# Query projection of an eight-head latent attention: rotary columns per head with their swap, or rotary chunks of all heads computed once ahead of the attention

## Chip, cores and metric

One core of one Trainium2 chip runs the whole kernel. The metric is the device time of one execution in microseconds, as the median of several runs.

## What is computed

A decoder block on one sequence of 1024 tokens and 1024 features: two token mixers beside each other (a latent attention with 8 heads and a gated linear attention with 4 heads), merged by sigmoid gates, then a SwiGLU feed-forward of 2816 columns. The change concerns the queries and the rotary key of the latent attention:

```python
q = (rmsnorm(c_q, norm_cq) @ w_uq).reshape(B, S, H, MLA_QK_DIM)      # 384 -> 8 heads x (64 plain + 32 rotary)
q_nope, q_rope = q[..., :64], q[..., 64:]
q_rope = apply_rope(q_rope, cos, sin)      # x1 cos - x2 sin, x2 cos + x1 sin
k_rope = apply_rope(k_rope, cos, sin)      # one rotary key of 32 columns for all heads
k = concat([k_nope, k_rope]); q = concat([q_nope, q_rope]) * 96 ** -0.5
s = causal_mask(q @ k.T); p = softmax(s); o = p @ v
```

## The kernel before, in words

**Products.** All activations are held transposed (features on partitions, tokens along the free axis, in two halves of 512). Every fp32 operand is kept as two fp32r parts, high and low. `split` makes the high part by a cast on ACT and the low part by a subtraction on POOL or DVE, and `mm3` (L134 to L138) makes a product of three matmuls: high x high, high x low, low x high. A matmul here has a moving side of 128x512. The big products (input projection, feed-forward) go through a Strassen-Winograd form in pairs of 128 columns: `weights` loads and splits a weight tile, `p_first` (L204) makes the first product and copies it to SBUF (ACT, L208), and `p_second`, `p_t2`, `p_t3`, `p_t4`, `p_t1`, `p_last` follow; between them plus and minus (DVE, L180 and L181) combine weights and results. A weight tile is split by ACT (L164) and DVE (L165).

**Pools that matter.** Rings of buffers hold these tiles: `st` has 5 buffers (products copied from PSUM and results on their way to DRAM), `wh` and `wl` have 4 each (split weights, and in this part the latents too), `wr` has 4 (raw weights from DRAM), and PSUM has 4 banks for each of two tags in the first part of the program.

**Before the attention.** `latents` (L751) loads the latents from DRAM, squares them (ACT), sums the squares by matmuls against ones (L772), and forms the inverse root on POOL (`rstd_of`, a power, L99). `token_rows` (L777) turns the result into a row that stands on all partitions: DVE makes a diagonal matrix (L782), and a matmul against ones spreads it (L785). The latent of the keys is multiplied by its rows and then split (L795 to L797). The latent of the queries is not multiplied by them: `q_split` (ACT L801, DVE L802) scales it by the gain alone and splits it at once, and the rows enter later, through `tab`.

**Queries.** A head's 96 query columns become 128: 64 plain ones, 32 rotary ones, and the 32 rotary ones again with their halves swapped (`load_uq`, L829, eight small casts and eight subtractions for each pair of heads). `qproj` (L844) makes one head and one half of the tokens by 9 matmuls, multiplies the PSUM bank by `tab` (DVE, L850: rows of the norm on the plain partitions, cosine times norm and signed sine times norm on the rotary ones), casts (ACT, L852) and subtracts (POOL, L853). The key has its rotary part summed and repeated to 64 partitions by `sel` (L870), so that the scores' contraction over 128 partitions adds cosine and sine terms. So the query projection is 8 chunks x 2 halves x 9 = 144 matmuls.

**Attention.** A loop over 32 items (head h, r from 0 to 3), each with 256 queries: `scores` (matmuls into `pss`, a mask matmul L931, a reduce on DVE L933, the exponential on ACT L935) and, one item later, `values` (transposes L950, copies ACT L953 and subtraction DVE L954, matmuls L959, then ACT L967 and DVE L968 into `zraw`, which is stored to `d_oa` at L971 once for each pair of heads). Item r has scores over 256(r+1) keys, so items r = 0 and 1 are small. Projections of later heads and parts of the gated mixer's output (`pj` banks) stand between the items.

**Order of the work.** Each engine runs its instructions in one fixed order. The order is not the written one: a list scheduler of the framework places the instructions of each engine by its own model, and pools of buffers set who must wait for whom. DMAs are issued by SP, in order as well.

Of the kernel before, what the change touches and what calls it, by code (L numbers as in the profile page):

```python
# [10 lines left out]
F32 = mybir.dt.float32  # L11
# [4 lines left out]
ALU = mybir.AluOpType  # L16
# [4 lines left out]
P = 128  # L21
# [27 lines left out]
def block_kernel(ctx, tc, x, positions, ln_mix, w_in, norm_cq, w_uq, norm_ckv, w_ukv, w_oa,  # L49
# [25 lines left out]
    d_oa = dram.tile([512, S], F32, name="d_oa")  # L75

# [451 lines left out]
    rot = rotp.tile([P, S], F32, name="rot", tag="rot", bufs=1)  # L528

    def rotary_table():  # L530
# [6 lines left out]
        nc.gpsimd.memset(frow[:, 1, :].rearrange("p (a r) -> p a r", r=64)[:, :, 32:48], -1.0)  # L537
# [5 lines left out]
        for half in range(2):  # L543
# [12 lines left out]
            nc.scalar.activation(rot[:, hs], ang, AF.Sin, scale=fcol[:, 1:2])  # L556
            nc.scalar.activation(kk, ang, AF.Abs)
            nc.vector.tensor_scalar(kk, kk, -1.0, math.pi / 2, ALU.mult, ALU.add)
            for r in (0, 64):
                nc.scalar.activation(rot[r:r + 32, hs], kk[r:r + 32], AF.Sin)  # L560
# [190 lines left out]
    def latents(row, n, name, each=None):  # L751
# [8 lines left out]
        for half in range(2):  # L760
            sq = None
            for c in range(n):
# [6 lines left out]
                if each:  # L769
                    each(c, half, raw[c][half])  # L770
# [17 lines left out]


    rs_kv, raws = latents(384, 2, "ck")  # L790
    ckh, ckl = ck_t
    for half, ps in enumerate(token_rows(rs_kv)):
        for c in range(2):
            cr = raws[c][half]
            nc.vector.scalar_tensor_tensor(cr, cr, g_ckv[:, c:c + 1], ps, ALU.mult, ALU.mult)  # L795
            nc.scalar.copy(ckh[half][c], cr)
            nc.vector.tensor_tensor(ckl[half][c], cr, ckh[half][c].bitcast(F32), ALU.subtract)  # L797
# [12 lines left out]

# [17 lines left out]

    def load_uq(hp):  # L829
        raw, hi, lo = wtiles(768)  # L830
        nc.sync.dma_start(raw[:, 0:576].rearrange("p (c n) -> p c n", c=3),
                          w_uq[0][:, hp * 192:(hp + 1) * 192].rearrange("(c p) n -> p c n", p=P))
        r4_ = raw[:, 0:576].rearrange("p (c h n) -> p c h n", c=3, h=2)
# [10 lines left out]
    def qproj(h, half, wq, newbank):  # L844
        hs = slice(half * HALF, (half + 1) * HALF)
# [741 lines left out]
```

## Time and profile before

| | |
|---|---|
| runs of the kernel before | 1490.79, 1494.8, 1496.61 us (median 1494.8) |
| the profiled execution | 1490.29 us, of which the span is 1488.6 us |
| PE busy | 1438.9 us (97% of the span) |
| DVE, ACT, POOL busy | 1021.8, 673.5, 491.5 us (69%, 45%, 33%) |
| DMA | 181.51 MB, mean 122 GB/s |
| granted TensorE clock, mean | 0.99 |

The span runs from the first to the last instruction of the profiled execution, and its own time is 1.7 us longer. Busy times are sums over the whole span. Since PE is busy nearly always, the places where it is not, and the number of its matmuls, are what a reader looks at first; a row of the trace then tells for one stretch which wait ended last.

### The profile page before, as it was taken

How to read it: one execution, taken by the hardware profiler on the slowest of the kernel's cores; microseconds unless marked ns; L12 is line 12 of the kernel's file. 1: busy time of each engine (PE TensorE's matmuls, PEld its weight loads, DVE VectorE, ACT ScalarE, POOL GpSimd, SP SyncE). 2: the span in 40 equal slices, each digit the busy share in tenths (PEclk: the TensorE clock that was granted, in tenths of full speed). 3: DMA queues.
4: the chain of work that ended last, by engine and by line, in shares of the span. 5: the costliest groups of instructions: out<-in, count | busy, mean ns of one | idle time of the engine just before them, and what ended most of it. 6: DMA issues, size and time to landing. Idle time of an engine off the chain costs nothing.

```text
span 1488.6 us, 20316 instructions
## 1 busy us (share of the span) xinstructions
PE 1438.9 (97%) x7422; PEld 1209.9 (81%) x7422; DVE 1021.8 (69%) x1453; ACT 673.5 (45%) x1333; POOL 491.5 (33%) x419
## 2 busy tenths in 40 slices
PE   7999999999979999999999899999999999999997
PEld 5899888778858888887899778888888888788886
DVE  4876786979665777574613876666666666886875
ACT  6542364535555776576303632222222223354454
POOL 3312231323122114235713465555555555100000
PEclk9999999999989999999999999999999999999999
DMA  8134324223421014358622223233323234952441
GB/s 237 43 116 128 114 92 147 86 79 109 146 93 59 1 44 143 104 173 282 250 77 86 85 73 105 94 104 107 99 100 106 93 106 148 398 202 94 139 158 57
DMA packets 123158, 181.51 MB, mean 122 GB/s; under 512 B 12898, under 2 KB 76915, under 8 KB 123059
## 3 DMA queue, kind: packets, MB, share of 16 engines
q1 hardware_dynamic: 122482, 178.38, 36.4%
q10 hardware_dynamic: 576, 1.84, 0.3%
q8 instruction: 58, 0.95, 0.3%
q14 instruction: 42, 0.34, 0.1%
HBM read 125.66 MB, written 54.53 MB: 121 GB/s over the span
## 4 chain that ended last, share of the span: by engine, by line
PE 50%; DVE 2%; DMA 1%; ACT 0%; POOL 0%; issue 0%; SPq 0%; DVEq 0%; POOLq 0%
PE psB L136 6%; PE psB L138 6%; PE psB L137 6%; PE psA L138 5%; PE psD L138 5%; PE psD L136 5%; PE psA L136 5%; PE psA L137 5%; PE psD L137 4%; PE psy L137 1%; PE psy L138 1%; PE psy L136 1%; DMA d_h<-h 1%; DVE UT L165 0%; DMA d_a<-R 0%; DMA xr<-d_a 0%
## 5 line engine op out<-in xcount | busy, mean ns | idle before, releaser
L165 DVE TENSOR_TENSOR ws<-wr,ws 128x512 fp32r<-128x512 f32 x135 | 136.6, 1022 | 11.4 <-ACT ws L164 10.9
L164 ACT CAST ws<-wr 128x512 fp32r<-128x512 f32 x157 | 94.0, 617 | 64.8 <-DVE wr L181 31.5
L99 POOL TENSOR_TENSOR rx<-rs_m,nhalf 128x1 f32<-128x1 f32 x24 | 14.8, 620 | 252.0 <-DVE rs_m L98 250.6
L136 PE MATMUL ps_mm<-u,ws 128*128 128x512 f32 x208 | 83.7, 402 | 11.8 <-ACT st L208 9.5
L165 POOL TENSOR_TENSOR ws<-sS,ws 128x512 fp32r<-128x512 f32 x44 | 70.8, 1619 | 67.8 <-ACT ws L164 67.8
L1225 ACT COPY p<-psA 128x512 f32<-128x512 f32 x22 | 12.9, 586 | 157.4 <-PE psA L138 157.4
L137 PE MATMUL ps_mm<-u,ws 128*128 128x512 f32 x208 | 83.2, 400 | 0.0
L138 PE MATMUL ps_mm<-u,ws 128*128 128x512 f32 x208 | 82.8, 401 | 0.0
L164 ACT CAST ws<-xr 128x512 fp32r<-128x512 f32 x73 | 45.1, 620 | 76.6 <-PE psD L138 35.1
L165 DVE TENSOR_TENSOR ws<-xr,ws 128x512 fp32r<-128x512 f32 x73 | 50.1, 688 | 33.7 <-ACT ws L164 33.6
L136 PE MATMUL psB<-UT,ws 128*128 128x512 f32 x176 | 69.2, 393 | 3.3 <-ACT UT L164 3.3
L629 POOL TENSOR_TENSOR X<-E,gk 128x512 f32<-128x512 f32 x28 | 45.6, 1639 | 79.1 <-ACT E L627 37.9
L137 PE MATMUL psB<-UT,ws 128*128 128x512 f32 x176 | 69.8, 397 | 0.2 <-POOL UT L165 0.2
L137 PE MATMUL psA<-UB,ws 128*128 128x512 f32 x176 | 69.7, 396 | 0.0
L138 PE MATMUL psA<-UB,ws 128*128 128x512 f32 x176 | 69.7, 396 | 0.0
L136 PE MATMUL psA<-UB,ws 128*128 128x512 f32 x176 | 69.5, 395 | 0.0
L138 PE MATMUL psB<-UT,ws 128*128 128x512 f32 x176 | 69.4, 394 | 0.0
L180 DVE TENSOR_TENSOR st<-st,ps_mm 128x512 f32<-128x512 f32 x75 | 51.3, 684 | 20.2 <-PE ps_mm L138 17.0
L954 DVE TENSOR_TENSOR ws<-pspt,ws 128x512 fp32r<-128x512 f32 (+1 forms) x80 | 49.6, 631 | 17.1 <-ACT ws L953 16.5
L935 ACT ACTIVATE u<-pss,nb 128x128 f32<-128x128 f32 (+3 forms) x64 | 47.7, 746 | 25.1 <-DVE nb L933 16.6
L164 ACT CAST ws<-sS 128x512 fp32r<-128x512 f32 x88 | 50.3, 619 | 17.9 <-DVE sS L1201 17.9
L136 PEld LDWEIGHTS ps_mm<-u,ws 128*128 128x128 f32 x208 | 39.6, 191 | 21.2 <-ACT st L208 10.0
(467 smaller groups left out, 4737.1 us busy)
## 6 DMA issues: line engine op xcount, KB each, us to landing
xr<-d_a SPq DMA_DIRECT2D x73, 256.0 KB, 3.0
wr<-in_w_in_dram SPq DMA_DIRECT2D x32, 512.0 KB, 4.4
wr<-in_ffn_w_gate_dram SPq DMA_DIRECT2D x22, 512.0 KB, 3.8
wr<-in_ffn_w_up_dram SPq DMA_DIRECT2D x22, 512.0 KB, 3.8
d_a<-p SPq DMA_DIRECT2D x20, 512.0 KB, 2.8
dr<-in_ffn_w_down_dram SPq DMA_DIRECT2D x14, 512.0 KB, 7.7
d_a<-R SPq DMA_DIRECT2D x10, 512.0 KB, 2.6
xt<-in_x_dram SPq DMA_DIRECT2D x8, 512.0 KB, 5.9
```

Of the source, the lines that this page charges most:

```text
L99: nc.gpsimd.tensor_tensor(dst, m, nhalf[:, :n], ALU.pow)
L136: nc.tensor.matmul(ps, ah, bh, start=first, stop=False, **kw)
L137: nc.tensor.matmul(ps, ah, bl, start=False, stop=False, **kw)
L138: nc.tensor.matmul(ps, al, bh, start=False, stop=last, **kw)
L164: nc.scalar.copy(dst[:, 0], src)
L165: (lo_eng or nc.gpsimd).tensor_tensor(dst[:, 1], src, dst[:, 0].bitcast(F32), ALU.subtract)
L180: plus = lambda d, x, y: nc.vector.tensor_tensor(d, x, y, ALU.add)
L629: nc.gpsimd.tensor_tensor(X, E, k, ALU.mult)
L935: nc.scalar.activation(pt[:, 0:w], ps[:, 0:w], AF.Exp, bias=bias, accum_out=sums[h // 2][:, t, e:e + 1])
L954: nc.vector.tensor_tensor(tl[:, 0:w], ps[:, 0:w], th[:, 0:w].bitcast(F32), ALU.subtract)
L1225: nc.scalar.copy(tt[:, 0:HALF], psA)
```

## The change

- The queries' latent is multiplied by its norm rows before it is split, as the keys' is (`normed`), and `q_split` goes.
- The rotary table has cosine and sine on all 128 partitions and is stored to DRAM (`d_rot`), and loaded back as `tab` after `p_second` of the last gate pair.
- `rope_queries` makes the rotary columns of all heads, once: 256 columns are two groups of four heads, times two halves, times 9 = 36 matmuls. Each of the four banks is multiplied by the cosine and by the sine (8 products on DVE), split (8 casts on ACT, 8 subtractions on POOL), and stored to DRAM (`d_qr`, 8 stores). It stands between `p_t2` and `p_t3` of the last gate pair.
- `qproj` now makes the 64 plain columns of two heads at once (8 x 9 = 72 matmuls in all) and fetches each head's rotary rows from `d_qr` by two DMAs of 32 partitions; the swap and its signs are in `sel` on the key side.
- The attention's items go pair by pair: both heads' r = 0 and 1, then both heads' r = 2 and 3.

```diff
+    d_rot = dram.tile([2, P, S], F32, name="d_rot")
+    d_qr = [[[dram.tile([P, S], F32, name=f"d_qr{g_}{half}{k}") for k in range(2)] for half in range(2)]
+            for g_ in range(2)]
...
+    def normed(rs, raws, g_, dst):
+        for half, ps in enumerate(token_rows(rs)):
+            for c, r in enumerate(raws):
+                cr = r[half]
+                nc.vector.scalar_tensor_tensor(cr, cr, g_[:, c:c + 1], ps, ALU.mult, ALU.mult)
+                nc.scalar.copy(dst[0][half][c], cr)
+                nc.vector.tensor_tensor(dst[1][half][c], cr, dst[0][half][c].bitcast(F32), ALU.subtract)
...
-    def q_split(c, half, cr):
-        nc.scalar.activation(cqh[half][c], cr, AF.Copy, scale=g_cq[:, c:c + 1])
-        nc.vector.scalar_tensor_tensor(cql[half][c], cr, g_cq[:, c:c + 1], cqh[half][c].bitcast(F32),
-                                       ALU.mult, ALU.subtract)
-
-    rs_q, _ = latents(0, 3, "cq", q_split)
+    rs_q, raws = latents(0, 3, "cq")
...
-    rq_ps = token_rows(sc_q)
+    normed(sc_q, raws, g_cq, cq_t)
...
+    def split_uq(src, n):
...
+        nc.scalar.copy(hi, src)
+        nc.gpsimd.tensor_tensor(lo, src, hi.bitcast(F32), ALU.subtract)
+        return w
...
-    def qproj(h, half, wq, newbank):
+    def rope_queries(newbank):
+
+        raw = wraw(768).rearrange("p (c h n) -> p c h n", c=3, h=8)
+        for c in range(3):
+            nc.sync.dma_start(raw[:, c], w_uq[0][c * P:(c + 1) * P, :].rearrange("p (h n) -> p h n", h=8)[:, :, 64:96])
+        hi, lo = split_uq(raw, 32)
+        for half in range(2):
+            hs = slice(half * HALF, (half + 1) * HALF)
+            for g_ in range(2):
+                ps = newbank()
+                fs = slice(g_ * P, (g_ + 1) * P)
+                for c in range(3):
+                    mm3(ps, hi[:, c, fs], lo[:, c, fs], cqh[half][c], cql[half][c], c == 0, c == 2)
+                for k in range(2):
+                    t = sttile()
+                    nc.vector.tensor_tensor(t, ps, tab[k][:, hs], ALU.mult)
+                    q = wslot().rearrange("p (e n) -> p e n", e=2)
+                    nc.scalar.copy(q[:, 0], t)
+                    nc.gpsimd.tensor_tensor(q[:, 1], t, q[:, 0].bitcast(F32), ALU.subtract)
+                    nc.sync.dma_start(d_qr[g_][half][k], q.rearrange("p e n -> p (e n)").bitcast(F32))
+
+    def qproj(hp, half, wq, newbank):
         ps = newbank()
         for c in range(3):
-            mm3(ps, wq[0][:, c, h % 2, :], wq[1][:, c, h % 2, :], cqh[half][c], cql[half][c], c == 0, c == 2)
-        q32 = wraw(HALF)
-        nc.vector.tensor_tensor(q32, ps, tab[h % 2][:, hs], ALU.mult)
-        q = uslot(0).rearrange("p (e n) -> p e n", e=2)
-        nc.scalar.copy(q[:, 0, :], q32)
-        nc.gpsimd.tensor_tensor(q[:, 1, :], q32, q[:, 0, :].bitcast(F32), ALU.subtract)
-        return q[:, 0, :], q[:, 1, :]
+            mm3(ps, wq[0][:, c], wq[1][:, c], cqh[half][c], cql[half][c], c == 0, c == 2)
+        for e in range(2):
+            h = 2 * hp + e
+            t = uslot(0)
+            q = t.rearrange("p (e n) -> p e n", e=2)
+            j = h % 4 * 32
+            for k in range(2):
+                r = ROT[e].start + 32 * k
+                nc.sync.dma_start(t[r:r + 32].bitcast(F32), d_qr[h // 4][half][k][j:j + 32, :])
+            rows = PLAIN[e]
+            nc.scalar.copy(q[rows, 0, :], ps[rows])
+            nc.vector.tensor_tensor(q[rows, 1, :], ps[rows], q[rows, 0, :].bitcast(F32), ALU.subtract)
+            qps[h, half] = q[:, 0, :], q[:, 1, :]
...
     p_second(w, out_gb)
+    tab = [uslot(0, F32) for k in range(2)]
+    for k in range(2):
+        nc.sync.dma_start(tab[k], d_rot[k])
...
-    nc.vector.tensor_tensor(krr, krr, rot[0:64], ALU.mult)
+    for k in range(2):
+        rows = slice(32 * k, 32 * k + 32)
+        nc.vector.tensor_tensor(krr[rows], krr[rows], tab[k][rows], ALU.mult)
...
     p_t2(w)
+    rope_queries(bank)
     p_t3(w)
...
-    items = [(h, r) for h in range(8) for r in range(4)]
+    items = [(2 * hp + e, 2 * half + r) for hp in range(4) for half in range(2) for e in range(2) for r in range(2)]
...
+        if n == 4:
+            kproj(1, bank_pj)
+        if n % 8 == 0 and n < 24:
+            wqs[n // 8 + 1] = load_uq(n // 8 + 1)
+        if n % 4 == 0 and n < 28:
+            hp, half = divmod(n // 4 + 1, 2)
+            qproj(hp, half, wqs[hp], bank_pj)
```

How the order of instructions moves is shown at three places. In the rows `ps_mm` is a PSUM bank, `ws` a split weight, `st` and `wr` tiles of the pools above, `wc` a raw latent and `c` its split parts.

**ACT, while the second-last gate pair begins, before.** The copy of the first product (L208) stands at the end:

```order
L801 ACTIVATE c_3658<-wc,g_cq 128x512
L164 CAST ws<-wr 128x512
L801 ACTIVATE c_3659<-wc,g_cq 128x512
L801 ACTIVATE c_3660<-wc,g_cq 128x512
L801 ACTIVATE c_3661<-wc,g_cq 128x512
L745 CAST wh<-wr 128x512
L164 CAST ws<-wr 128x512
L208 COPY st<-ps_mm 128x512
```

The same place on ACT in the changed kernel, where L795 is the cast of `normed`, L168 the weights' cast and L212 the copy:

```order
L795 CAST c_3597<-wc 128x512
L168 CAST ws<-wr 128x512
L795 CAST c_3598<-wc 128x512
L168 CAST ws<-wr 128x512 x3
L212 COPY st<-ps_mm 128x512
L274 ACTIVATE st<-ps_mm 128x512
L795 CAST c_3666<-wc 128x512
```

The splits of the queries' latent (c_3656 to c_3661 before, c_3666 to c_3671 now) and the cast of the up-projection's weights (L745) have moved from ahead of the copy to behind it.

**PE, at the start of the rotary products, changed kernel.** The first row is the last of five groups of 12 matmuls of the gate pairs that now stand between the spreading of the norm rows and the rotary key (L906, which is L870 before):

```order
L142 MATMUL ps_mm<-v_483,ws 128x512
L906 MATMUL ps_g<-wr,sel 128x512 x2
L140 MATMUL ps_mm<-c_3666,wh 128x512
L141 MATMUL ps_mm<-c_3672,wh 128x512
L140 MATMUL ps_mm<-c_3666,wh 128x512
L141 MATMUL ps_mm<-c_3672,wh 128x512
L140 MATMUL ps_mm<-c_3669,wh 128x512
L141 MATMUL ps_mm<-c_3675,wh 128x512
```

Before, the rotary key followed the norm rows at once, and the gate pair went on:

```order
L785 MATMUL ps_g<-st,ones 128x512 x2
L870 MATMUL ps_g<-wr,sel 128x512 x2
L136 MATMUL ps_mm<-k_631,ws 128x512
L137 MATMUL ps_mm<-k_631,ws 128x512
L138 MATMUL ps_mm<-k_631,ws 128x512
```

All 36 rotary matmuls stand in one block, whose first rows take all four banks in turn with the high weights; behind the block come the 12 matmuls of `p_t3`.

**ACT, behind that block, changed kernel.** L836 casts the rotary weights, L863 the rotary products, and L168 the weights of `p_t3` and what follows it:

```order
L274 ACTIVATE st<-ps_mm 128x512
L274 ACTIVATE st<-st 128x512
L916 CAST u_3947<-ps_g 64x512 x2
L916 CAST u_3948<-ps_g 64x512 x2
L836 CAST wh<-wr 128x768
L863 CAST ws<-st 128x512 x8
L168 CAST ws<-wr 128x512 x4
L748 CAST k_4152<-wr 128x512 x2
```

Before, in the same part of the program, ACT had these rows (L882 copies norm rows into `tab`, L884 is L916 above):

```order
L882 COPY u_3919<-ps_g 64x512 x2
L164 CAST ws<-wr 128x512
L270 ACTIVATE st<-st 128x512
L884 CAST u_3921<-ps_g 64x512 x2
L882 COPY u_3920<-ps_g 64x512
L208 COPY st<-ps_mm 128x512
```

So all eight casts of rotary products are put ahead of the weight splits that `p_t3` needs.

## Rows read from the trace of the kernel before

**Rows 1.** The page's head and engine totals: busy us, share, instructions.

```profile
span 1488.6 us, 20316 instructions
PE 1438.9 (97%) x7422; PEld 1209.9 (81%) x7422; DVE 1021.8 (69%) x1453; ACT 673.5 (45%) x1333; POOL 491.5 (33%) x419
```

**Rows 2.** Waits, 380 to 430 us: us in total, times, longest.

```profile
PE ps_mm L136 <- ACT st L208: 8.8, 1, 8.8
```

**Rows 3.** PE's timeline: start, duration, [idle before].

```profile
409.81 0.95 PE L772 MATMUL ps_g<-ones,st 128*128 128x1 f32 x8
419.54 0.79 PE L136 MATMUL ps_mm<-u,ws 128*128 128x512 f32 x1 [8.78 <-ACT st L208]
...
424.30 1.88 PE L785 MATMUL ps_g<-st,ones 128*128 128x512 f32 x4
426.11 1.98 PE L870 MATMUL ps_g<-wr,sel 64*128 64x512 f32 x4
```

**Rows 4.** Windows: length, busy of PE (count), granted clock, DMA share, GB/s.

```profile
414.00:419.00 5.00, 0.00 (x0) 0.50 0.34 105
420.00:423.00 3.00, 3.00 (x8) 0.50 0.61 175
```

**Rows 5.** ACT's timeline in front of that copy.

```profile
410.07 0.62 ACT L164 CAST ws<-wr 128x512 fp32r<-128x512 f32 x1 [0.58 <-PE ps_mm L138]
...
412.86 1.94 ACT L801 ACTIVATE c<-wc,g_cq 128x512 fp32r<-128x512 f32 x3
416.88 0.62 ACT L745 CAST wh<-wr 128x512 fp32r<-128x512 f32 x1 [2.08 <-DMA wr<-in_mla_w_ukv_dram]
418.39 0.62 ACT L164 CAST ws<-wr 128x512 fp32r<-128x512 f32 x1 [0.89 <-DVE c L802]
418.91 0.58 ACT L208 COPY st<-ps_mm 128x512 f32<-128x512 f32 x1
```

**Rows 6.** PE's timeline in the last gate pair.

```profile
430.66 0.39 PE L138 MATMUL ps_mm<-k,ws 128*128 128x512 f32 x1
...
441.64 0.39 PE L138 MATMUL ps_mm<-v,ws 128*128 128x512 f32 x1
```

**Rows 7.** POOL's powers of line 99: ns min/median/max, start.

```profile
L99 POOL TENSOR_TENSOR ckrs<-rs_m,nhalf x1: 1635/1635/1635, 398.5 to 398.5; 128x8 f32<-128x8 f32 x1
L99 POOL TENSOR_TENSOR cqrs<-rs_m,nhalf x1: 5879/5879/5879, 413.3 to 413.3; 128x8 f32<-128x8 f32 x1
```

**Rows 8.** DVE's timeline beside the second of these powers.

```profile
417.62 0.73 DVE L802 SCALAR_TENSOR_TENSOR c<-wc,g_cq,c 128x512 fp32r<-128x512 f32 x1
419.24 0.17 DVE L807 TENSOR_SCALAR sc_q<-cqrs 128x8 f32<-128x8 f32 x1 [0.88 <-POOL cqrs L99]
```

**Rows 9.** DMAs of line 405 (64 KB each, runs of 128 bytes), issue to landing.

```profile
DMA to landing us min/median/max: 2.9/3.2/3.5
```

**Rows 10.** DMA issues on the page: KB each, median us to landing.

```profile
d_a<-p SPq DMA_DIRECT2D x20, 512.0 KB, 2.8
...
d_oa<-zraw SPq DMA_DIRECT2D x3, 512.0 KB, 3.7
...
xf<-d_a SPq DMA_DIRECT2D x4, 256.0 KB, 6.3
```

**Rows 11.** POOL's subtraction of line 853, ns min/median/max.

```profile
L853 POOL TENSOR_TENSOR u<-wr,u x16: 1272/1287/1302, 470.6 to 645.4; 128x512 fp32r<-128x512 f32 x16
```

**Rows 12.** Windows before and in the attention: busy (count) of PE, PEld, DVE, ACT, POOL; clock.

```profile
425.00:470.00 45.00, 45.00 (x189) 35.14 (x188) 23.25 (x36) 21.38 (x44) 3.88 (x9) 1.00 0.29 95
470.00:676.00 206.00, 201.29 (x1275) 172.68 (x1274) 143.46 (x233) 138.46 (x323) 63.20 (x66) 1.00 0.28 89
```

**Rows 13.** DVE, a reduce in the first item.

```profile
472.38 0.67 DVE L933 TENSOR_REDUCE nb<-pss 128x1 f32<-128x128 f32 x2 [0.42 <-PE pss L931]
```

**Rows 14.** ACT, exponentials and a copy in the first items.

```profile
473.92 0.37 ACT L935 ACTIVATE u<-pss,nb 128x128 f32<-128x128 f32 x1
...
477.18 0.48 ACT L953 CAST ws<-pspt 128x384 fp32r<-128x384 f32 x1
```

More of the change, by code (lines that the diff above doesn't have):

```diff
@@ L749, in block_kernel, with latents @@
     g_cq = gain_cols(norm_cq[0], 3, "g_cq")
-    def latents(row, n, name, each=None):
+    def latents(row, n, name):
         rs = small.tile([P, NT], F32, name=f"{name}rs", tag=f"{name}rs", bufs=1)
@@ L827, in kproj @@
                 nc.vector.tensor_tensor(kl[e][rows, hs], ps[rows], kh[e][rows, hs].bitcast(F32), ALU.subtract)
+    def split_uq(src, n):
+        k = src.shape[2] * n
+        w = wslot()[:, 0:6 * k].rearrange("p (e c n) -> p e c n", e=2, c=3) if k == P else None
+        if w is None:
+            w = [t[:, 0:3 * k].rearrange("p (c n) -> p c n", c=3) for t in wtiles2()]
+        else:
+            w = [w[:, e] for e in range(2)]
+        hi, lo = (t.rearrange("p c (h n) -> p c h n", n=n) for t in w)
+        nc.scalar.copy(hi, src)
+        nc.gpsimd.tensor_tensor(lo, src, hi.bitcast(F32), ALU.subtract)
+        return w
@@ L829, in load_uq @@
     def load_uq(hp):
[L830 to L831 removed]
+        raw = wraw(576)
+        nc.sync.dma_start(raw.rearrange("p (c n) -> p c n", c=3),
                           w_uq[0][:, hp * 192:(hp + 1) * 192].rearrange("(c p) n -> p c n", p=P))
[L833 to L835 removed]
@@ L836, in load_uq @@
-        for e in range(2):
-            n0, r0 = (0, 64) if e == 0 else (64, 0)
-            for (dst, src, w) in ((n0, 0, 64), (r0, 64, 32), (r0 + 32, 80, 16), (r0 + 48, 64, 16)):
-                nc.scalar.copy(h4[:, :, e, dst:dst + w], r4_[:, :, e, src:src + w])
-                nc.gpsimd.tensor_tensor(l4[:, :, e, dst:dst + w], r4_[:, :, e, src:src + w],
-                                        h4[:, :, e, dst:dst + w].bitcast(F32), ALU.subtract)
-        return h4, l4
-    def qproj(h, half, wq, newbank):
-        hs = slice(half * HALF, (half + 1) * HALF)
+        return split_uq(raw.rearrange("p (c h n) -> p c h n", c=3, h=2)[:, :, :, 0:64], 64)
@@ L860, in block_kernel @@
     p_second(w, out_gb)
+    tab = [uslot(0, F32) for k in range(2)]
+    for k in range(2):
+        nc.sync.dma_start(tab[k], d_rot[k])
     krr = wraw(1024)[0:64]
     nc.sync.dma_start(krr, d_c[640:704, :])
-    nc.vector.tensor_tensor(krr, krr, rot[0:64], ALU.mult)
-    nc.gpsimd.tensor_tensor(sel, ident[0:64, 0:32].unsqueeze(1).broadcast_to([64, 4, 32]),
-                            ident[0:64, 32:64].unsqueeze(1).broadcast_to([64, 4, 32]), ALU.add)
+    for k in range(2):
+        rows = slice(32 * k, 32 * k + 32)
+        nc.vector.tensor_tensor(krr[rows], krr[rows], tab[k][rows], ALU.mult)
+    for g_ in range(4):
+        for i in range(2):
+            j = 16 * (i ^ (g_ % 2))
+            nc.gpsimd.tensor_tensor(sel[:, g_, 16 * i:16 * i + 16], ident[0:64, j:j + 16],
+                                    ident[0:64, 32 + j:48 + j], ALU.subtract)
     kr_ps = []
@@ L875, in block_kernel @@
     up_weights(1, wv_h, wv_l)
-    tab = [uslot(0, F32) for e in range(2)]
     Kh[0], Kl[0] = ([uslot(0) for e in range(2)] for x in "hl")
@@ L879, in block_kernel @@
         hs = slice(half * HALF, (half + 1) * HALF)
-        for e in range(2):
-            nc.vector.tensor_tensor(tab[e][ROT[e], hs], rot[ROT[e], hs], rq_ps[half][ROT[e]], ALU.mult)
-            nc.scalar.copy(tab[e][PLAIN[e], hs], rq_ps[half][PLAIN[e]])
         for e in range(2):
@@ L906, in block_kernel @@
     kproj(0, bank)
-    qps[0, 0] = qproj(0, 0, wqs[0], bank)
+    qproj(0, 0, wqs[0], bank)
     pp.close()
```

29 lines of the change are left out of this document (6 added, 23 removed).

## Prediction

> **What bounds the kernel now.** I read the page's totals first: PE is busy for 1438.9 of 1488.6 us [rows 1], so what counts is how many matmuls it runs and where it stands still. Next the waits around the place of the change: between 380 and 430 us PE waits once at length, 8.8 us for a copy on ACT [rows 2]. PE's timeline puts that wait ahead of the second product of the second-last gate pair, at 419.54 us [rows 3]. The windows show what it costs beyond itself: the granted clock stands at 0.50 while PE is idle and still at 0.50 from 420 to 423 us, the lower of the two levels, 1.2 GHz [rows 4]. The 12 matmuls from 419.54 to 424.30 take 4.76 us, where the undisturbed interval of such a matmul is 0.229 us (48 of them between the two starts of [rows 6], 10.98 us), so 12 would take 2.75. The wait costs 8.8 + 2.0 = 10.8 us.
>
> ACT's timeline says why the copy is late: the engine has three splits of the queries' latent to do, then a weight cast that waits 2.08 us for a DMA, then a cast that waits for DVE, and only then the copy [rows 5]. Last, the attention from 470 to 676 us: PE is busy for 201.29 of 206 us at full clock, with DVE and ACT at 143 and 138 us, so PE bounds it too, but by less [rows 12].
>
> **The change, term by term.** The sum is made against the profiled execution, 1490.3 us; the median of the runs, 1494.8, stands 4.5 above it.
>
> (a) *Matmuls.* 144 of the query projection become 72 + 36 = 108. The removed ones lie on PE, which is the bound: 36 x 0.229 = 8.2 us less [rows 6].
>
> (b) *The old wait.* In the new order the six splits and the weight cast stand behind the copy. ACT then reaches it after three weight casts from 410.07 on, at about 0.52 us from start to start (418.39 to 418.91 in [rows 5]): 411.6, and 0.58 more for the copy itself, 412.2. PE's sums start at 409.81 and take 0.95 [rows 3], so about 1.5 us of wait is left, and I take the clock to stay up. Now the rows of the norm are wanted sooner, by the multiplication of the latent: the power on POOL, then DVE, then the spreading matmuls. Before, the power took 5.88 us [rows 7], and its result reached DVE 0.88 us after a run of eight DVE instructions, the last of them at 417.62, had ended [rows 8]. So the row reads as a power that is held up while DVE works on two tiles of SBUF. After the change three such DVE instructions stand between the power's input and its result, not eight; at about 0.62 each and 0.9 behind them that is 2.8 us, and PE waits about 0.8 us for the spreading. If the power takes its old 5.88 whatever DVE does, 3.1 to 3.3 us more. Term: -10.8 + 1.5 + 0.8 = -8.5, with -5.2 as its other end.
>
> The Trainium skill, page "SBUF — State Buffer", section "Who interferes with whom", states that a DVE instruction with two inputs in SBUF and a GpSimd instruction that reads SBUF shut each other out for a whole instruction. By that rule the sum is as above; by the bare 5.88 us it would be 3.3 us higher; the trace agrees as far as the 0.88 us goes.
>
> (c) *A wait for the rotary weights.* PE reaches the first rotary matmul after 60 matmuls and two small products behind the spreading of the norm rows: 60 x 0.229 + 2 x 0.93 = 15.6 us (0.93 each from [rows 3], where two spreadings and two key products run from 424.30 to about 428.05). The weights' three loads go into a raw buffer that DVE must first have read, as the last of some 23 instructions it has from that point (six products and six subtractions for the latent, plus and minus of the gate pairs, two products for the key, weight splits): at 0.62 us each about 14.5 us. The loads come as runs of 128 bytes. The nearest row is a 64 KB load in such runs, 3.2 us to landing [rows 9]; three loads of twice that size issue one after the other, so 4 to 5 us from the first issue; a slow load of 256 KB takes 6.3 [rows 10], which I keep as the far end. The cast of 128x768 is added at 0.8 us, an estimate from 0.62 for 512 columns [rows 5]. So the weights are there at 14.5 + 4.9 + 0.8 = 20.2, and PE waits 4.6 us. A wait of this length I take to bring the lower clock as the 8.8 us did, for another 2.0: 6.6. Ends: 3 (a shorter load, the clock kept) and 8.
>
> The Trainium skill, page "DMA: Bandwidth & Descriptors", section "Specifications", states that transfers need pieces of at least 512 bytes for full rate; this speaks against these loads. The sum by the slow end would be 1.4 us higher; no run here has shown this load.
>
> (d) *A wait ahead of `p_t3`.* The four banks give eight products, and POOL subtracts for 1.29 us each [rows 11]. The first bank is whole 15 matmuls into the block, nine of them at the low clock: 5.2 us. Product and cast add 1.3, so POOL starts at 6.5. The `st` ring has four free buffers, so the eighth product waits for the fourth subtraction, 11.7, and its cast ends at 12.9. Behind the eight casts stand the weight casts of `p_t3`, which also want a buffer that the third store to DRAM gives back: third subtraction 10.4, landing 2.8 [rows 10], 13.2. Cast and subtraction bring the weights to about 14.5. PE ends the block at 5.2 + 21 x 0.229 = 10.0: a wait of 4.5 us, with 2.0 for the clock, 6.5. Ends: 3 and 8.
>
> (e) *Attention.* Its projections shrink by 71 matmuls, counted in (a) together with the 35 more that now stand ahead of it. The order of items puts four small ones side by side in each pair of heads. One item's chain is two reduces 0.67 [rows 13], exponentials of 0.37 and more with their sums, about 0.8, transposes 0.3, a copy 0.48 [rows 14] and a subtraction about as long, 2.7 us in all, against 1.8 us of PE work in a neighbouring item of the smallest kind. Bursts of nine projection matmuls (2.1 us) stand near most of these, so I take 0.5 us for each of four groups, and little for `zraw`, whose store takes 3.7 us [rows 10] and now has one DVE instruction fewer in front of the next write. Together +2.0; ends 0 and 12.
>
> Nothing: the 16 attention-time transfers more for the rotary rows, and the eight stores (4 MB), hide under a DMA share of 0.28 [rows 12]; without that cover each would show its 2.8 us or so. ACT loses the small casts and DVE gains about as much as it loses.
>
> **Sum:** -8.2 - 8.5 + 6.6 + 6.5 + 2.0 = -1.6, so 1488.7 for an execution like the profiled one, and **1493** for the median. The saved matmuls and the removed wait are paid back by two new waits.
>
> **Rivals.** *A, the new waits are short.* If the weights' load finds a free buffer earlier, or the order that I read leaves PE enough, each of (c) and (d) is 2 us or less and the clock stays up. For it: the same engines go fast elsewhere, and only one long wait in the old stretch brought the clock down. Against it: the load stands behind a DVE list that is itself behind the norm rows, and POOL's eight subtractions are 10.3 us against a block of 8.2. Time: -8.2 - 8.5 + 2 + 2 + 1 = -11.7, near 1483 for the median.
>
> *B, slower: small items bound by their chain.* Four small items in a row leave PE without large items to work on while a reduce, an exponential and a copy follow each other. If each exposes about 1 us, four groups of four give 16 us, in place of 2: 1507. It decides against the change once the attention's extra is above 3.6 us (+2.0 and the 1.6 of gain), and beyond what a measurement can tell from 11 us on. For it: PE's spare time in the attention is only 4.7 us now, with large items beside each small one [rows 12]. Against it: the projections between the items, and DVE and ACT at 70%.
>
> *C, the rotary rows come late.* If the products are not far enough ahead of the attention, the first scores wait for store and load, 2.8 + 4 us. By the new order some 126 matmuls, 29 us, lie between; it adds 3 us at most, to 1496.
>
> **Numbers.** Forecast 0.48, A 0.30, B 0.17, C 0.05. What a measurement of this kernel can tell from no change is 0.5%, 7.5 us. Faster by more than that is A and a little of the forecast's lower end (both waits at 3): 0.33. Slower is B and the forecast's upper end, with the power at 5.88 us and both waits at 8: 0.18. The range reaches to A's time and halfway to B's: 1481 to 1502.
>
> **What would show it.** In the profile after: the wait of PE for the copy of the first product is 2 us or less; PE idles ahead of the first rotary matmul for the cast of the rotary weights, and again ahead of `p_t3` for ACT or DVE, each 3 to 6 us with the clock at 0.5 behind; the attention lasts about 191 us in place of 206; PE has 36 matmuls fewer. I am wrong if PE goes through the rotary block without a stop, if the power keeps 5.9 us, or if PE's idle time in the attention is several times 4.7 us.

## Result: slower by half a per cent

The changed kernel takes 1503.0 us (median of 9 runs, 1498.54 to 1507.79) against 1495.6 us of the kernel before (9 runs, 1490.79 to 1497.87): ratio 1.0053, with a 95% interval from 1.0040 to 1.0066. The forecast was 1493, in a range up to 1502. The profiled execution of the changed kernel, 1504.15 us, is 13.9 us longer than that of before, 1490.29; the latter was faster than all nine timed runs, so the profiles differ by more than the medians. Lengths read from one profile are worth a few us, not less.

The page after, with the totals that answer to [rows 1]:

```profile
span 1502.4 us, 20318 instructions
PE 1444.4 (96%) x7386; PEld 1211.3 (81%) x7386; DVE 1034.3 (69%) x1464; ACT 672.3 (45%) x1308; POOL 470.6 (31%) x391
```

PE has 36 matmuls fewer and is busy for 5.5 us more. Matmuls that take longer can do that, and the place is seen in the waits of PE from 380 to 480 us (line, what it waited for, us in total, times, longest), where before had the one row of [rows 2]:

```profile
PE ps_mm L140 <- ACT ws L168: 4.3, 1, 4.3
PE ps_mm L140 <- ACT wh L836: 3.7, 1, 3.7
PE ps_mm L142 <- DVE ws L169: 2.0, 1, 2.0
PE ps_mm L140 <- ACT st L212: 1.5, 1, 1.5
```

The wait of 8.8 us has become 1.5 (last row), and three others are new. PE's timeline, start and duration, with [idle before], shows them around the rotary block (438.81 to 449.66) and `p_t3` (from 454.37):

```profile
413.12 0.50 PE L140 MATMUL ps_mm<-u,ws 128*128 128x512 f32 x1 [1.50 <-ACT st L212]
...
417.57 1.88 PE L786 MATMUL ps_g<-st,ones 128*128 128x512 f32 x4
...
433.13 1.98 PE L906 MATMUL ps_g<-wr,sel 64*128 64x512 f32 x4
438.81 0.79 PE L140 MATMUL ps_mm<-c,wh 128*128 128x512 f32 x1 [3.70 <-ACT wh L836]
...
449.66 0.40 PE L142 MATMUL ps_mm<-c,wl 128*128 128x512 f32 x1
454.37 0.50 PE L140 MATMUL ps_mm<-v,ws 128*128 128x512 f32 x1 [4.31 <-ACT ws L168]
454.71 0.58 PE L141 MATMUL ps_mm<-v,ws 128*128 128x512 f32 x1
457.29 0.80 PE L142 MATMUL ps_mm<-v,ws 128*128 128x512 f32 x1 [2.00 <-DVE ws L169]
...
461.66 0.40 PE L140 MATMUL ps_mm<-k,ws 128*128 128x512 f32 x1
```

Behind each wait the matmuls are slow. The 36 of the block take 449.66 + 0.23 - 438.81 = 11.1 us in place of 8.2; ten of `p_t3` take 4.4 (457.29 to 461.66) in place of 2.3; even the 12 behind the short wait take 4.45 (413.12 to 417.57) in place of 2.75. Together 6.7 us. The windows of the same stretch (length; busy time of PE, its weight loads, DVE, ACT and POOL; then the granted clock, 0.50 being the lower level as in [rows 4] and a value between 0.50 and 1.00 a window that holds both; DMA share, GB/s):

```profile
415.00:420.00 5.00, 5.00 (x16) 3.36 (x15) 4.10 (x8) 1.19 (x2) 0.00 (x0) 0.78 0.19 65
...
440.00:445.00 5.00, 5.00 (x15) 3.85 (x14) 0.00 (x0) 0.00 (x0) 0.66 (x1) 0.55 0.30 105
...
455.00:460.00 5.00, 3.00 (x7) 2.16 (x7) 3.53 (x3) 1.52 (x3) 1.69 (x2) 0.50 1.01 385
```

Up to the first scores, at 489.0 us, the changed kernel is 18.0 us behind (471.0 before). Some 8 of them are the 36 rotary matmuls, which now run there. The attention, from the first scores to the last product with the values, is where they should have come back. The same columns, first before, then after:

```profile
471.00:675.40 204.40, 200.04 (x1271) 171.79 (x1269) 142.33 (x231) 137.69 (x321) 62.25 (x66) 1.00 0.28 90
```

```profile
489.00:689.90 200.90, 192.11 (x1211) 163.41 (x1209) 145.44 (x233) 135.41 (x300) 33.74 (x27) 0.98 0.35 107
```

These two windows do not hold the same work. The change took 72 projection matmuls out (126 before, 54 now; of the loop's 135 and 63, nine run ahead of the first scores in both), but PE's count falls only by 60: in the kernel before, the last of the twelve products of the gated mixer (12 matmuls, 676.06 to 679.13 us) stands behind the last product with the values, in the changed kernel it stands ahead of it. So I also take the length from the first scores to the first matmul of the next part (`psy`), which holds all twelve products in both:

```profile
471.01:680.24 209.23, 203.34 (x1283) 174.10 (x1282) 145.25 (x235) 141.69 (x329) 63.39 (x67) 1.00 0.29 93
```

```profile
489.02:692.03 203.01, 192.35 (x1212) 163.53 (x1210) 145.85 (x234) 137.20 (x304) 35.87 (x29) 0.98 0.34 107
```

72 matmuls fewer, 16.5 us at 0.229, make it 6.2 us shorter. PE stands for 10.7 us in place of 5.9, and the clock, at 1.00 throughout before, falls twice, behind waits of 1.6 and 1.5 us:

```profile
493.00:497.00 4.00, 4.00 (x17) 3.06 (x18) 2.36 (x5) 1.83 (x5) 0.00 (x0) 0.66 0.23 66
581.00:585.00 4.00, 3.74 (x19) 3.65 (x20) 3.63 (x7) 3.09 (x8) 2.93 (x3) 0.57 0.62 182
```

What lies behind that, from the first matmul of the next part to the end of the span, takes 810.4 us against 808.4.

### The profile page after: what moved, and what is told of

It is laid out like the page before. It is cut to its first block, busy times and chain, and to the rows that moved or that the text cites. A ratio compares the mean times of both kernels' runs of the same rounds, so it can differ in the third digit from the quotient of the medians.

```text
span 1502.4 us, 20318 instructions
## 1 busy us (share of the span) xinstructions
PE 1444.4 (96%) x7386; PEld 1211.3 (81%) x7386; DVE 1034.3 (69%) x1464; ACT 672.3 (45%) x1308; POOL 470.6 (31%) x391
## 4 chain that ended last, share of the span: by engine, by line
PE 63%; DVE 7%; DMA 4%; ACT 3%; issue 2%; POOL 0%; SPq 0%; DVEq 0%; ACTq 0%; POOLq 0%
PE psB L140 6%; PE psB L141 6%; PE psB L142 6%; PE psA L141 4%; PE psA L140 4%; PE psA L142 4%; PE psD L140 4%; PE psD L141 4%; PE psD L142 4%; PE ps_mm L140 2%; PE ps_mm L141 2%; PE ps_mm L142 2%; PE acc L992 2%; PE psy L142 1%; PE psy L140 1%
## 5 line engine op out<-in xcount | busy, mean ns | idle before, releaser
L169 DVE TENSOR_TENSOR ws<-wr,ws 128x512 fp32r<-128x512 f32 x135 | 133.3, 997 | 15.3 <-ACT ws L168 14.8
L168 ACT CAST ws<-wr 128x512 fp32r<-128x512 f32 x157 | 94.0, 617 | 65.0 <-DVE wr L185 30.8
L103 POOL TENSOR_TENSOR rx<-rs_m,nhalf 128x1 f32<-128x1 f32 x24 | 13.9, 583 | 253.4 <-DVE rs_m L102 251.9
L168 ACT CAST ws<-xr 128x512 fp32r<-128x512 f32 x73 | 45.0, 620 | 77.4 <-PE psD L142 35.1
L987 DVE TENSOR_TENSOR ws<-pspt,ws 128x512 fp32r<-128x512 f32 (+1 forms) x80 | 49.8, 632 | 13.1 <-ACT ws L986 12.2
L168 ACT CAST ws<-sS 128x512 fp32r<-128x512 f32 x88 | 50.2, 619 | 17.9 <-DVE sS L1233 17.9
L966 DVE TENSOR_REDUCE nb<-pss 128x1 f32<-128x128 f32 (+3 forms) x64 | 48.1, 751 | 12.8 <-PE pss L964 12.2
L992 PE MATMUL acc<-ws,v 128*128 128x256 f32 (+1 forms) x320 | 52.7, 293 | 4.3 <-DVE zraw L1001 2.1
```

The costliest lines, as they stand in the source:

```text
L103: nc.gpsimd.tensor_tensor(dst, m, nhalf[:, :n], ALU.pow)
L168: nc.scalar.copy(dst[:, 0], src)
L169: (lo_eng or nc.gpsimd).tensor_tensor(dst[:, 1], src, dst[:, 0].bitcast(F32), ALU.subtract)
L966: nc.vector.tensor_reduce(bias, ps[:, 0:w], AX.X, ALU.max, negate=True)
L987: nc.vector.tensor_tensor(tl[:, 0:w], ps[:, 0:w], th[:, 0:w].bitcast(F32), ALU.subtract)
L992: nc.tensor.matmul(acc[:, a:256], V[j][:, h, :], src[:, jj * 256:jj * 256 + 256 - a], start=j == 0 and k == 0, stop=j == nj - 1 and k == 1 ...
```

## Experiments

Each kernel was timed beside the kernel before on the same chip, so ratios are to that, with 95% intervals. "Attention" is the length from the first scores to the last product with the values, "to next part" the one to the first matmul of the next part, both from the profile of each kernel. My expectations use the first. It leaves out the last mixer product, 12 matmuls or 2.7 us, in the kernel before, in "latent normed first", in "75 matmuls left out" and in the kernels with 16 products (up to 30 matmuls in the late ones), and holds it in the others; the second always holds them all.

| kernel | median us | ratio | attention us | to next part us |
|---|---|---|---|---|
| before | 1495.6 | 1 | 204.4 | 209.2 |
| changed | 1503.0 | 1.0053 [1.0040, 1.0066] | 200.9 | 203.0 |
| old order of items | 1502.3 | 1.0056 [1.0037, 1.0075] | 198.6 | 202.6 |
| rotary products behind T1 | 1485.4 | 0.9938 [0.9923, 0.9953] | 199.4 | 201.5 |
| rotary products behind T3 | 1497.0 | 1.0024 [1.0009, 1.0038] | 200.5 | 202.5 |
| before, latent normed first | 1488.6 | 0.9967 [0.9952, 0.9982] | 205.2 | 210.0 |
| before, new order of items | 1502.0 | 1.0051 [1.0034, 1.0069] | 213.7 | 217.6 |
| before, 75 matmuls left out | 1483.7 | 0.9926 [0.9911, 0.9942] | 197.0 | 201.8 |
| behind T1, old order of items | 1488.3 | 0.9958 [0.9944, 0.9973] | 198.7 | 202.5 |
| behind T1, all 16 mixer products inside | 1483.2 | 0.9923 [0.9909, 0.9937] | 207.4 | 212.1 |
| behind T1, half of the rotary products inside | 1487.5 | 0.9950 [0.9936, 0.9965] | 202.4 | 204.7 |
| behind T1, 16 products, spread | 1486.6 | 0.9946 [0.9927, 0.9965] | 209.4 | 214.0 |
| behind T1, 35 matmuls left out | 1484.6 | 0.9936 [0.9915, 0.9956] | 195.6 | 198.4 |
| behind T1, 16 products, late | 1491.9 | 0.9984 [0.9969, 0.9999] | 210.1 | 218.8 |
| the same, first weights early | 1485.9 | 0.9945 [0.9930, 0.9960] | 204.2 | 214.6 |

### The waits ahead of the attention

**Rotary products behind T1.**

```diff
     p_t2(w)
-    rope_queries(bank)
     p_t3(w)
     p_t4(w, out_gb, True)
     p_t1(w, out_gb)
+    rope_queries(bank)
     p_last(w, out_gb)
```

> The changed kernel with the rotary products written behind the gate pair's product T1 in place of ahead of T3 (36 more matmuls ahead of them, about 8.2 us). Theory 'two waits': PE's waits of 3.7 us for the rotary weights and of 4.3 + 2.0 us for the weights of T3 go, with the low clock behind them (some 2.3 us each); -11 to -15, so 1488 to 1492. Rival 'late rows': the rotary rows now reach DRAM later and the first scores wait for them, or the drain of eight products holds up the values' projection: half of the gain or less, 1496 to 1501.

Measured: 1485.4 us. By the two ratios this is 1.15% or some 17 us below the changed kernel, more than the 11 to 15 expected. Of PE's waits from 405 us to the first scores only two are left:

```profile
PE ps_mm L140 <- ACT st L212: 1.5, 1, 1.5
PE pss L140 <- DVE u L881: 0.3, 1, 0.3
```

The first scores start at 470.4 us in place of 489.0, and the rows of `d_qr` are there in time (the 0.3 us are for DVE). Of these 18.6 us the waits ahead of the block and of `p_t3` with the slow matmuls behind them are 3.7 + 2.8 and 4.3 + 2.0 + 2.1, 14.9 in all. Another 1.7 is the clock behind the first wait, which stays up in this profile, 0.4 a shorter wait just ahead of the attention, and 1.8 were there before the stretch began (the sums start at 408.84 us, not 410.67).

The drain itself is no faster here. POOL's subtractions take as long as before, and ACT's next weight cast still waits for a store to `d_qr`. PE does not meet this, since 24 matmuls of the values' projection, whose weights lie ready, come between the block and the 12 matmuls of `p_last`, which want those weights. POOL, ACT, and PE at the start of the 24 and inside the 12:

```profile
443.86 10.14 POOL L864 TENSOR_TENSOR ws<-st,ws 128x512 fp32r<-128x512 f32 x8 [3.93 <-ACT ws L863]
...
452.31 0.62 ACT L168 CAST ws<-wr 128x512 fp32r<-128x512 f32 x1 [0.65 <-DMA d_qr<-ws]
...
448.43 0.40 PE L140 MATMUL ps_mm<-wh,c 128*128 128x512 f32 x1
...
454.60 0.50 PE L142 MATMUL ps_mm<-u,ws 128*128 128x512 f32 x1
```

**Rotary products behind T3**, the same edit with the line one place after `p_t3`.

> The changed kernel with the rotary products written directly behind T3, 12 matmuls (2.75 us) later than in the change. Theory 'two waits': the weights of T3 are split ahead of the rotary casts, so the wait of 4.3 + 2.0 us and the low clock behind it go, while the wait for the rotary weights keeps about 1 of its 3.7 us, and the clock stays up: 1486 to 1489. Rival 'ring': the eight products still hold the st and weight buffers when the next product of the gate pair wants them, so a wait of 3 to 6 us moves behind the block: 1492 to 1497.

Measured: 1497.0 us, the rival. The four longest waits of PE ahead of the attention in this kernel:

```profile
PE ps_mm L140 <- ACT ws L168: 4.4, 1, 4.4
PE ps_mm L142 <- DVE ws L169: 1.6, 1, 1.6
PE ps_mm L140 <- ACT st L212: 1.5, 1, 1.5
PE ps_mm L140 <- ACT wh L836: 1.3, 1, 1.3
```

The wait for the rotary weights fell from 3.7 to 1.3 us, by about the 12 matmuls that now stand ahead. The pair of 4.3 and 2.0 stayed (4.4 and 1.6) and hit the next product of the gate pair, which follows the block at once. So it does not hang on `p_t3`: it meets whoever wants freshly split weights right behind the block. By the ratios the step from the change to this kernel is worth some 4 us, and the step from here to the block behind T1 some 13, each to within 3. By profile the first is 2.4 of wait and 2.8 of clock, which stays at 1.00 behind the wait of 1.3.

Why the drain holds, in the changed kernel: POOL subtracts without a pause until 456.69, ACT's casts for `p_t3` wait for stores to `d_qr`, and the first of DVE's two subtractions behind them takes 2.9 us. The timelines of POOL, ACT and DVE in turn:

```profile
446.67 10.02 POOL L864 TENSOR_TENSOR ws<-st,ws 128x512 fp32r<-128x512 f32 x8 [6.01 <-ACT ws L863]
...
453.70 0.62 ACT L168 CAST ws<-wr 128x512 fp32r<-128x512 f32 x1 [0.57 <-DMA d_qr<-ws]
456.38 0.62 ACT L168 CAST ws<-wr 128x512 fp32r<-128x512 f32 x1 [2.06 <-DMA d_qr<-ws]
...
454.35 3.49 DVE L169 TENSOR_TENSOR ws<-wr,ws 128x512 fp32r<-128x512 f32 x2 [1.87 <-ACT ws L168]
```

### The old wait alone

**Before, latent normed first**: the kernel before with `normed` for the queries' latent as in the change, and `tab` filled with the plain table and ones.

```diff
-            nc.vector.tensor_tensor(tab[e][ROT[e], hs], rot[ROT[e], hs], rq_ps[half][ROT[e]], ALU.mult)
-            nc.scalar.copy(tab[e][PLAIN[e], hs], rq_ps[half][PLAIN[e]])
+            nc.vector.tensor_copy(tab[e][ROT[e], hs], rot[ROT[e], hs])
+            nc.gpsimd.memset(tab[e][PLAIN[e], hs], 1.0)
```

> The kernel before with one part of the change alone: the queries' latent is multiplied by its norm rows before the split, and tab holds the plain rotary table and ones. Kernel before 1495.6 us. Theory 'old wait': PE's wait of 8.8 us for the copy of the first product falls to 1 to 2 us and the clock stays up, -8.5 (-7 to -10), so 1487. Rival 'norm chain': the split latent is now late for the first query projection or DVE's six instructions more hold up the gate pair: -3 to +2, so 1493 to 1498.

Measured: 0.9967, so 5 us, between the two. The wait did not fall to 1.5 us here but to 2.9 in two parts, one of 2.3, and the clock fell behind it. The first scores start 4.6 us earlier than before (466.4). The wait shrinks as it should, by less than I had written; that this comes of an order of instructions other than that of the change is not shown.

### The attention

**The changed kernel with the old order of items.**

```diff
-    items = [(2 * hp + e, 2 * half + r) for hp in range(4) for half in range(2) for e in range(2) for r in range(2)]
+    items = [(h, r) for h in range(8) for r in range(4)]
...
-        if n % 4 == 0 and n < 28:
-            hp, half = divmod(n // 4 + 1, 2)
+        if n % 8 in (0, 6) and n < 30:
+            hp, half = (n // 8, 1) if n % 8 == 0 else (n // 8 + 1, 0)
             qproj(hp, half, wqs[hp], bank_pj)
```

> The changed kernel with its attention items in the order of before (head by head, r = 0 to 3); the projection of the next pair's first half moves from n = 4 (mod 8) to n = 6. Changed kernel 1503.0 us, its attention (first scores to last values) 201 us, against 188 to 189 us if it had lost nothing but 71 matmuls of 0.229 us. Theory 'order': four small items side by side uncover their own chains; with the old order the attention takes about 190 us, and the time is 1492 (-9 to -12). Rival 'cover': the 71 matmuls that left the attention had filled PE while the softmax ran, so the old order does not help: attention 198 to 201 us, time 1500 to 1503.

Measured: no change in time, attention 198.6 us, and to the next part 202.6 against 203.0. By itself that is against 'order'.

**The kernel before with the new order of items**, its projections still one for every two items.

> The kernel before with only the order of the attention's items changed to that of the change (both heads' r = 0 and 1, then both heads' r = 2 and 3); all 144 projection matmuls stay. Kernel before 1495.6 us, attention 205 us. Theory 'order': the small items cost 8 to 12 us here too, 1504 to 1508. Rival 'cover': with all projection matmuls still between the items the order costs 0 to 4 us, 1496 to 1500.

Measured: 1.0051, so 7.6 us, just under what 'order' promised, and an attention of 213.7 us. That is 9.3 more than before, but with the 12 mixer matmuls inside; to the next part it is 8.3 more. So here the order does cost about 8 us. The two runs agree only if the cost of the order hangs on how many projection matmuls stand between the items.

**Before, matmuls left out.**

```diff
+        if newbank is bank:
+            for c in range(3):
+                mm3(ps, wq[0][:, c, h % 2, :], wq[1][:, c, h % 2, :], cqh[half][c], cql[half][c], c == 0, c == 2)
+        else:
+            mm3(ps, wq[0][:, 0, h % 2, :], wq[1][:, 0, h % 2, :], cqh[half][0], cql[half][0], True, False)
+            nc.tensor.matmul(ps, wq[0][:, 2, h % 2, :], cqh[half][2], start=False, stop=True, skip_group_check=True)
```

> The kernel before, order of items unchanged; of the nine matmuls of each of the 15 query projections inside the attention, five are left out (75 in all, so the queries lack most of their latent's contributions); every other instruction stays. Attention of the kernel before 204.4 us from first scores to last values, time 1493.5 to 1495.6. Theory 'cover': the attention has a length of its own of about 198 to 201 us that these matmuls only fill, so they give back 4 to 6 us: time 1488 to 1491. Rival 'price': each is worth its 0.229 us there too, 17 us: attention 187 us, time 1477; what the changed kernel lost in its attention would then come from the row loads and the new drains of the projections.

Measured: attention 197.0 us, 7.4 shorter (and 7.4 to the next part), not 17. Since the first of the 15 projections runs ahead of the first scores, 70 of the 75 matmuls, 16.0 us, lie in that window. The time fell by 11 us, between the theories; even the far end of its interval, 13 us, is short of the 17.2 for all 75 (the profiles, of which that of before lies under its timed runs, differ by 6). Nothing else changed in this kernel: no row loads, no new drains, no new order. So 70 matmuls fewer by themselves leave 201.8 us to the next part, near the 203.0 of the changed kernel with its 72. Its window:

```profile
471.00:668.00 197.00, 188.59 (x1200) 160.47 (x1200) 141.96 (x231) 137.86 (x321) 62.38 (x66) 0.99 0.30 93
```

DVE and ACT do the same work as before in less time, and PE stands more: what it waited for inside, in this kernel,

```profile
PE acc L963 <- DVE zraw L972: 3.1, 2, 2.6
PE pspt L954 <- DVE ws L958: 2.9, 5, 1.3
```

are the steps of an item's own chain on DVE. **The same with the rotary products behind T1**, 35 matmuls left out of the seven projections inside in the same manner.

> The changed kernel with the rotary products behind T1, and five of the nine matmuls left out in each of the seven query projections inside the attention (35 matmuls, 8.0 us at 0.229; the queries lack most of their latent's contributions). Attention with all of them 199.4 us, time 1485.4. If an attention of about 198 us is set by the items' own chains (theory 'cover' in its plainest form): attention 197 to 199 us, time 1483 to 1485. If in the new order of items these matmuls are still worth their price: attention 191 to 192 us, time 1477 to 1478.

Measured: to the next part 198.4 us against 201.5, and 30 of the 35 matmuls lie in that window, so 0.10 us for each in place of 0.229 (0.13 by the attention column), and no difference in time that the intervals can tell. That is 'cover', though not in its plainest form: the length still gives a little.

**Both repairs.**

> The changed kernel with both repairs: rotary products behind T1, and the items in the order of before. Rotary products behind T1 alone gave 1485.4 us with an attention of 199.4 us; the old items alone left the time where it was, attention 198.6 against 200.9 us. If the attention has a length of its own, the old order gives 0 to 3 us here too: 1483 to 1486. If the order of the items is a cost of its own that was hidden by something else in that run, 5 to 10 us: 1476 to 1480.

Measured: 0.9958 against 0.9938 without the old order, attention 198.7 us, 202.5 to the next part against 201.5. Nothing is gained, so the order is no cost here.

Five runs put matmuls into the attention. **All 16 mixer products inside** (two in each of the last four items):

> The changed kernel with the rotary products behind T1 and all 16 products of the gated mixer's output inside the attention, two in place of one in each of the last four items (48 matmuls, 11.0 us, come from behind the attention into it). Theory 'cover': these matmuls fill PE where the softmax holds it up, so the attention grows by 3 to 6 us and the part behind it shrinks by 11: 1478 to 1481. Rival: the last items are already full of work, and nothing is gained: 1484 to 1487.

**Half of the rotary products inside**, those of heads 4 to 7 in front of the loop:

> The changed kernel with the rotary products of heads 0 to 3 behind T1 and those of heads 4 to 7 (18 matmuls, 4.1 us) at the start of the attention, where PE waits some 2 us for the first exponentials. Theory 'cover': they cost little there, so 1 to 4 us faster than with all behind T1 (1485.4): 1481.5 to 1484.5. Rival: their four products and casts stand on DVE and ACT ahead of the first items' softmax, or the projections' one bank holds up the second query projection: 0 to 4 us slower, 1485 to 1489.

**Spread**, one product in each of items 18 to 29 and two in each of the last two:

> The changed kernel with the rotary products behind T1 and all 16 products of the gated mixer inside the attention, spread: one in each of items 18 to 29, two in the last two, with the second half's input loaded at item 24. Two in each of the last four items gave 1483.2 us, one in each 1485.4. If the attention has room for matmuls wherever they are spread: 1480 to 1483. If its last stretch is bound by PE anyway: 1483 to 1486.

**Late**, items 22 to 31, and then the same with the first weights loaded at item 17:

> The changed kernel with the rotary products behind T1; the first half of the gated mixer's input is loaded at item 20 in place of 16 (there its products stand on DVE in the middle of a group of small items), and its 16 output products stand in items 22 to 31, two each in the small items 24 and 25 and in the last four. Reference runs: 1485.4 us without the move and with 12 products inside, 1483.2 with 16. If small items are where the attention has room: the wait of about 2 us near the third pair's start goes and products in items 24 and 25 cost little, 1478 to 1482. If it makes no difference where they stand: 1482 to 1485.

> The kernel of the run before, with the first output product's weights loaded at item 17 as in the change, not at 20 (there PE waited 6.9 us for their cast, with the low clock behind). If that wait was all that went against it, the wait and some 2 us of clock come off 1491.9: 1481 to 1484, and the small items have room as theory 'cover' says. If the products take their price there too: 1485 to 1488.

Measured: the 48 mixer matmuls, 11.0 us, lengthened the stretch to the next part by 10.6 us, so they paid nearly their full price inside; the time was 1483.2 us. (The attention column grows by 8.0 only since it again leaves out the last product, and so holds 36 of the 48.) With half of the rotary products in front of the loop, 18 matmuls more, 4.1 us, lengthened it by 3.2, and PE waited 2.8 us for DVE (`u`) just ahead of the first scores; 1487.5 us in all, as the rival had it. Spread, the 16 products gave 1486.6 us and 12.4 us more to the next part. The late form ran into a wait of its own making:

```profile
PE pj L140 <- ACT ws L122: 6.9, 1, 6.9
```

Without it the kernel took 1485.9 us, with 13.1 us more to the next part. But for the late form with its wait, none is clear of the 1485.4 us with the rotary products behind T1 alone. So the reverse of 'cover', that small items have free room for work brought in, did not show: in the new order and with the rotary products behind T1, matmuls brought into the attention cost 0.17 us each (18 of them) to 0.22 and more (48), and those left out of it give back 0.10. The fastest kernel that ran is the one with all 16 products inside, 0.9923; it beats both kernels of the change, and is not told apart from the one with the rotary products behind T1.

## Why the prediction was wrong

The step that failed is the price of the matmuls taken out of the attention: (a) counted them at 0.229 us each as work on the bound, and (e) took back only 2.0 us. 72 matmuls fewer, 16.5 us, made this stretch 6.2 us shorter, so 10.3 us were lost there. The sum was -1.6 us on the profiled execution; the profiles differ by +13.9. Step by step:

- **(a), the matmuls.** The count is right (7422 to 7386). The price of 0.229 us holds ahead of the attention. It failed for those taken out of the attention, which I counted as work on the bound because PE is busy there for 97% [rows 12]. Busy was not bound: the stretch to the next part is shorter by 6.2 us (the change), 6.7 (its old order) and 7.4 (before with 70 of its matmuls left out, nothing else changed), against 16.5, 16.5 and 16.0.
- **(b), the old wait.** Right: 1.5 us of wait predicted and measured. The power on POOL took 2.0 us in place of 5.9, as the reading of [rows 7, 8] had it, and no wait for the spreading shows in place of the predicted 0.8. Wrong for the profiled execution was that the clock would stay up, 1.7 us; in seven of the ten other profiles with this same wait it did, and why not here is not shown. By profile the term is -10.8 + 1.5 + 1.7 = -7.6, for -8.5.
- **(c), the rotary weights.** Right in place and size: 3.7 us of wait for 4.6, 2.8 of clock for 2.0; 6.5 for 6.6. The landing took 3.4 to 3.7 us per load.
- **(d), the drain.** Place and first wait right, 4.3 us for 4.5, with POOL's eight subtractions in 10.0 us as its cause. The term was too small: a second wait of 2.0 us stood behind the first, because the next weight's subtraction on DVE took far longer than the 0.6 us I had given it. 4.3 + 2.0 + 2.1 of clock = 8.4 for 6.5. By the runs (c) and (d) together are worth some 17 us, where these profiles have 14.9.
- **(e), the attention.** Here the failed step shows. I gave it +2.0, with 12 as the far end; by the profiles, to the next part, it is 203.0 - (209.2 - 16.5) = +10.3 (72 matmuls went, not the 71 that I wrote). Its cause was not the one that I had named for the far end: with the old order of items it is still 202.6 - 192.7 = 9.9, and leaving 70 matmuls out of the kernel before loses 201.8 - (209.2 - 16.0) = 8.6 without any other change. In the changed kernel PE's longer standing is 4.8 of the 10.3, and the lower clock, by its share of windows of 4 us, about 3.4 (an estimate); I had no term for a clock that falls inside the attention. The signs that I had set were half right: the attention did not come down to 191 us, but PE's idle time in it did not reach several times 4.7 us either.

These add to -8.2 - 7.6 + 6.5 + 8.4 + 10.3 = 9.4. The changed kernel was 0.9 us late already ahead of the stretch (its sums start at 410.67, not 409.81), a new wait just ahead of the attention takes 0.7, and the part behind it 2.0: 13.0 of the 13.9. In the nine other kernels with the same work in that last part it takes 809.6 to 812.2 us, so there the profile of before, with 808.4, is the short one. The timed runs bear out the size of (e): with both waits gone the change gains 9.3 us, where (a) and (b) alone promise 16.7; 7.4 are missing, and that kernel's profile shows 8.8 lost in the attention.

**Rivals.** A (short waits) failed, as the order had said. B came closest in time (1507) and was right that the attention holds the large extra, but wrong in its mechanism for this kernel: putting the items back gave nothing. It is right for another kernel, the one before with all its matmuls (8.3 us more with the new order). C did not occur.

In medians the miss is 9 us, not 15, since the profiled execution of before, from which I summed, lies some 5 us under the median of its runs. The two new waits decide the sign, and the drain is the larger of them: with the rotary products behind T1 the same change is 0.6% faster, though its attention is as long.

**Open.** What sets the attention's length of about 200 us is not shown step by step; the waits point at an item's chain through DVE and ACT, and no run shortened that chain. Why the new order costs about 8 us with the loop's 135 projection matmuls and nothing with 63 is not shown.

## To carry to other kernels

A stretch where one engine is 97% busy can give back less than half of what is taken out of it (here 6 to 7 us of 16): before counting removed work there at full price, leave some of it out and see what the stretch gives back. Compare such stretches only between points that enclose the same work. A block that drains through a slow engine and shared rings hits whoever next needs those rings. Here the drain took 10 us in either place; it cost PE 6 us and the clock where freshly split weights were wanted next, and nothing where 24 matmuls with ready weights came between.

## What I had not expected of the hardware

- The granted clock fell behind a wait of 1.5 us, and not always. Eleven profiles have this wait in the same place, for the same copy. In four of them (the change, and behind T1: all 16 products, 35 left out, late) the 12 matmuls behind it took 4.38 to 4.45 us; in the other seven, most of them also behind T1, 2.87 to 2.90, with the clock at 1.00. So the place of the rotary products does not decide it.
- A subtraction of two SBUF tiles on DVE, 0.69 us by its median, took up to 2.9 us while POOL ran its subtractions one after another: it began at 454.35 and ended 0.5 us after the last of POOL's, at 457.24. The line's durations (min/median/max, ns) in the changed kernel:

```profile
L169 DVE TENSOR_TENSOR ws<-wr,ws x135: 674/692/2885, 65.4 to 1267.2; 128x512 fp32r<-128x512 f32 x135
```

I had used the rule on DVE and GpSimd shutting each other out (the Trainium skill, page "SBUF — State Buffer", section "Who interferes with whom") for POOL's power only. The timelines agree with it in the other direction too, and there it would explain the second wait: with the products behind T3 and behind T1, too, the first such subtraction on DVE ends 0.5 to 0.6 us after the last of POOL's. But one subtraction on POOL takes 1.25 us, and 2.9 us are more than a wait for one of them and DVE's own 0.69 make, so DVE was held through more than one; the rule as I used it speaks of one.
